# A hybrid recurrence, attention and gating block: scores on row halves of the array, normalisation after all heads, and sums that stay in PSUM

## The chip, the cores and the metric

The kernel runs on one core of a Trainium2 chip. The metric is the device time of one launch in microseconds (us). The kernel before takes 1037.99 us, the median of three runs (1035.18 to 1039.12). The profiled execution took 1038.81 us; its span, from the first to the last recorded instruction, is 1037.0 us. The engines are TensorE (PE, with its weight loads as PEld), VectorE (DVE), ScalarE (ACT), GpSimd (POOL) and SyncE (SP), which here only issues transfers.

## The reference

One layer of a backbone over 512 latent tokens `x` and 256 context tokens, all of width 1024 and in float32. Both are modulated by a small network of the condition vector, and one projection makes the inputs of three branches:

```python
px = split_proj(modulate(x, sh_x, sc_x), w_in, b_in)          # 512 x 12288; pc: the same of ctx
# A: a convolution of width 4, then a gated linear recurrence over tokens in both directions
h_a = rglru_scan(conv(px[0]), ..., reverse=False) + rglru_scan(conv(px[0]), ..., reverse=True)
# B: differential attention, 8 heads, two maps (m) of 64 channels each, rotary q and k
s = einsum('bqhmd,bkhmd->bhmqk', q, k) * 64 ** -0.5           # k: 512 latent + 256 context
p = softmax(s)
o = einsum('bhqk,bkhe->bqhe', p[:, :, 0] - lam * p[:, :, 1], v)
attn = o * rsqrt(mean(o * o) + eps) * g * 0.2                 # mean over a head's 128 channels
# C: spatial gating of u = px[6] by layer_norm(v = px[7])
sgu = u * (w_s @ layer_norm(v) + b_s)
y = sum(sigmoid(gate_i) * ((branch_i * silu(g_i)) @ w_branch[i]) for i in A, B, C)
x_new = layer_norm(alpha * x + gt_x * (y @ w_out))
```

## The kernel before

**Numbers.** Every projection is done to float32 accuracy out of three passes of a faster format: an operand is kept as a rounded part (hi) and the rest (lo), and `mm3` (lines 57 to 64) issues hi by hi, hi by lo and lo by hi for each of 8 slices of 128 along the contraction. Its three matmuls are the lines L62, L63 and L64 of the profile. The modulated latents `xhl` and the context `chl` stay in SBUF in this form. Making hi is a cast on ScalarE, lo a subtraction on VectorE or GpSimd.

**Weights.** They stream through in units. SyncE issues a transfer of 512 KB into one of three buffers `raw`, ScalarE casts it to hi (L121), and GpSimd during attention, VectorE otherwise, subtracts to lo (L122), into one of four slots `w`. A channel-major unit (`cm`) is 128 output channels by all 1024 inputs and takes one slot: its product has channels in partitions and 512 tokens in columns, 24 matmuls of 512 columns. A token-major unit (`tm`) is 256 output channels and takes two slots: tokens lie in partitions, and each of four token tiles takes 24 matmuls of 256 columns into one accumulator. A unit's slot is filled again by `pump` after a unit is used.

**Order.** TensorE's instructions run in the order in which the code issues them. For the other engines and the transfers a scheduler places each instruction by its estimate of when it can start, with priority for what stands under `high_priority`; `order` and `issue_after` tie a few of ScalarE's to one another. PSUM is used as two accumulators of 512 columns (`acc`) and three tiles of 1024 (`big`).

**Stages.** Head and modulation (0 to 62 us); the values of the first heads and attention (62 to 412); the recurrence of branch A together with branch B's output projection (412 to 645); branch C's `sv` (645 to 703); then A's output, `u`, the spatial gating, C's output, the gate row `gr`, and `out` with the last layer norm.

**Attention** has 32 steps, 8 heads by 4 tiles of 128 queries. A step issues `scores` (L705: for each map a `big` tile of 128 queries by 768 keys), `softmax` (row maxima L715 on VectorE, exponentials L720 on ScalarE, the second of them written over its own score tile in PSUM), `combine` (L730, the difference of both maps), the transposes of the step before (L735) with their split (L746, L748), and in between projections from a table `fill`: k, the context's k, q, v and the gate `gb` of later heads. For each head `values` multiplies with v and `rms` normalises: `ms` is the mean of the squares over 128 channels, by a matmul with a matrix of 1/128, and L762 to L764 take logarithm, exponential and product. Small work for the next head (the rotary product, whose one factor GpSimd multiplies, and the splits of q and k) waits in a list of chores, and `drain` issues some of it in each step.

For the scores, q and k of a head lie as 128 partitions, 64 for each map. `qd` and `kd` hold for each map hi in one half of the partitions and lo in the other; q's hi and lo are copied into the other half as well, by a transfer that GpSimd issues. So two matmuls with a contraction of 128 give the three products of a map.

**Recurrence.** Group g of 128 channels takes `xa` (512 latents) and `xac` (256 context tokens) into the padded row `pad`, a convolution on VectorE (`xc`), its split (`xch`, `xcl`), four gate products `ri` with sigmoids, the decay and scans, then `ga`; `branch_a` writes the result to DRAM (`pa_d`). Branch B's split output `hsB` is multiplied in `merge_b` (`y1`), gated by `merge_gate` (`gt1`). After the loop `pa` is read back for branch A.

**Branch C.** `proj_tokens` makes `sv` and `u`: a product of 24 matmuls, and then a sum with the bias on VectorE (L1041) that empties the accumulator. The bias is a row copied to all partitions by a transfer.

## Time and profile before

| | |
|---|---|
| Median of three runs | 1037.99 us (1035.18 to 1039.12) |
| Profiled execution | 1038.81 us, span 1037.0 us |
| Mean granted clock of TensorE | 0.972 of full speed |
| Busy: TensorE, VectorE, ScalarE, GpSimd | 94%, 64%, 51%, 15% of the span |

A row of a timeline gives the start, the duration and the operation, outputs before the arrow; in brackets stands how long the engine had been idle and who released it. A matmul's duration includes its way through a pipeline, so what it costs is read from the distance between two starts. The granted clock is a share of full speed: 1.0 is 2.4 GHz, 0.5 is 1.2.

### The profile page before, as it was taken

What the parts mean: (1) busy time and instruction counts of PE and PEld (TensorE: products, weight loads), DVE (VectorE), ACT (ScalarE), POOL (GpSimd) and SP (SyncE); (2) the same over time, 40 slices, a digit from 0 to 9 for tenths busy, and PEclk for the clock granted to TensorE, in tenths of its full rate; (3) what the DMA queues carried; (4) which work ended last, traced back from release to release, by engine and by line L of the source; (5) the groups of instructions that cost most, each with busy time, mean ns of one, the idle gap of its engine ahead of it and who ended that gap; (6) DMA issues with size and microseconds to landing.
All of it is one profiled execution on the core that took longest, in us unless ns stands there. A gap on an engine that the chain in (4) does not pass through costs nothing.

```text
span 1037.0 us, 14225 instructions
## 1 busy us (share of the span) xinstructions
PE 974.0 (94%) x5719; PEld 844.0 (81%) x5719; DVE 663.6 (64%) x1024; ACT 526.1 (51%) x741; POOL 155.7 (15%) x117
## 2 busy tenths in 40 slices
PE   5997799989989998999999999599999999999996
PEld 4796688878878886888888888598889988888896
DVE  4479788788788663787777776348433356424567
ACT  3145856647647796897777794213231234332221
...
GB/s 299 296 103 84 62 61 21 42 101 21 41 102 21 41 102 70 43 51 102 102 102 92 82 92 92 189 107 132 95 99 82 82 102 82 236 171 145 98 61 82
DMA packets 148184, 103.41 MB, mean 100 GB/s; under 512 B 3629, under 2 KB 143382, under 8 KB 148118
## 3 DMA queue, kind: packets, MB, share of 16 engines
...
q10 hardware_dynamic: 144, 0.10, 0.0%
...
## 4 chain that ended last, share of the span: by engine, by line
PE 66%; DVE 16%; ACT 10%; DMA 4%; issue 3%; SPq 1%; POOL 0%; POOLq 0%; ACTq 0%; DVEq 0%
PE y L62 4%; PE gt L62 4%; PE gt L64 4%; PE gt L63 4%; PE y L64 4%; PE y L63 4%; DVE mxn L715 2%; DVE e L730 2%; DVE kd L565 2%; PE out L62 1%; PE u L62 1%; PE u L64 1%; PE u L63 1%; PE out L64 1%; PE out L63 1%
## 5 line engine op out<-in xcount | busy, mean ns | idle before, releaser
L121 ACT CAST w<-raw 128x1024 fp32r<-128x1024 f32 x96 | 99.7, 1044 | 83.5 <-PE y L64 20.0
L122 DVE TENSOR_TENSOR w<-raw,w 128x1024 fp32r<-128x1024 f32 x71 | 86.4, 1222 | 66.9 <-ACT w L121 66.9
L62 PE MATMUL gt<-xhl,w 128*128 128x512 f32 x192 | 75.6, 394 | 1.3 <-ACT pad L865 1.3
L63 PE MATMUL gt<-xhl,w 128*128 128x512 f32 x192 | 74.8, 390 | 0.0
L64 PE MATMUL gt<-xhl,w 128*128 128x512 f32 x192 | 74.8, 390 | 0.0
L705 PE MATMUL s<-kd,qdq 128*128 128x512 f32 (+1 forms) x256 | 58.7, 368 | 15.6 <-ACT e L720 6.0
L122 POOL TENSOR_TENSOR w<-raw,w 128x1024 fp32r<-128x1024 f32 x25 | 61.0, 2445 | 67.4 <-ACT w L121 67.4
L705 PEld LDWEIGHTS s<-kd,qdq 128*128 128x128 f32 x256 | 44.5, 196 | 27.1 <-issue 12.7
L715 DVE TENSOR_REDUCE mxn<-s 128x1 f32<-128x768 f32 x64 | 58.3, 949 | 7.5 <-PE s L705 7.5
L720 ACT ACTIVATE e<-s,mxn 128x768 f32<-128x768 f32 x32 | 28.8, 900 | 50.9 <-DVE mxn L715 50.8
...
L62 PEld LDWEIGHTS gt<-xhl,w 128*128 128x128 f32 x192 | 36.1, 188 | 9.1 <-ACT pad L865 1.5
L64 PEld LDWEIGHTS gt<-xhl,w 128*128 128x128 f32 x192 | 36.0, 188 | 7.7
L63 PEld LDWEIGHTS gt<-xhl,w 128*128 128x128 f32 x192 | 36.1, 188 | 7.0
...
L730 DVE SCALAR_TENSOR_TENSOR e<-s,sm,e 128x768 f32<-128x768 f32 x32 | 32.6, 1017 | 6.5 <-ACT e L723 5.7
L54 ACT CAST vh<-v 128x128 fp32r<-128x128 f32 x48 | 12.4, 264 | 42.7 <-PE v L64 19.5
L842 ACT ACT_TABLE_LOAD x25 | 32.1, 1283 | 0.5
L62 PE MATMUL xa<-xhl,w 128*128 128x512 f32 x64 | 26.3, 411 | 4.8 <-ACT pad L865 4.8
L748 DVE TENSOR_TENSOR wtl<-t,wth 128x768 fp32r<-128x768 f32 x32 | 30.3, 950 | 0.6 <-ACT wth L746 0.5
L723 ACT ACTIVATE e<-e,sm 128x768 f32<-128x768 f32 x32 | 29.9, 934 | 0.2 <-DVE sm L722 0.2
L842 ACT ACTIVATE rt<-ri,colB 128x770 f32<-128x770 f32 x32 | 27.7, 906 | 2.5 <-PE ri L64 1.8
...
## 6 DMA issues: line engine op xcount, KB each, us to landing
raw<-in_w_in_dram SPq DMA_DIRECT2D x96, 512.0 KB, 3.9
raw<-in_w_branch_dram SPq DMA_DIRECT2D x24, 512.0 KB, 4.0
...
qdq<-qdq POOLq DMA_DIRECT2D x16, 256.0 KB, 3.2
adg<-in_w_ada_dram SPq DMA_DIRECT2D x8, 512.0 KB, 6.6
raw<-in_w_out_dram SPq DMA_DIRECT2D x8, 512.0 KB, 3.4
xtok<-in_x_dram SPq DMA_DIRECT2D x4, 512.0 KB, 5.7
ada<-in_w_ada_dram SPq DMA_DIRECT2D x4, 512.0 KB, 5.9
```

Of the source, the lines that this page charges most:

```text
L62: PE.matmul(ps, ah, bh, start=(first and i == 0), stop=False)
L63: PE.matmul(ps, ah, bl, start=False, stop=False)
L64: PE.matmul(ps, al, bh, start=False, stop=(last and i == n - 1))
L121: S.copy(h, raws[j])
L122: state["lo"].tensor_tensor(l, raws[j], f(h), ALU.subtract)
L705: PE.matmul(sp[:, sl], qds[h][:, 2 * m + j, qs], kds[h][:, m, sl], start=(j == 0), stop=(j == 1))
L715: V.tensor_reduce(mxn[:, m:m + 1], sps[m][:, 0:TA], mybir.AxisListType.X, ALU.max, negate=True)
L720: S.activation(e, sps[m][:, 0:TA], AF.Exp, bias=mxn[:, m:m + 1], accum_out=sm[:, m:m + 1])
L723: S.mul(es[i][0], es[i][0], sm[:, 0:1])
L730: V.scalar_tensor_tensor(e0, e1, sm[:, 1:2], e0, op0=ALU.mult, op1=ALU.add)
L748: V.tensor_tensor(wts[h][1][:, :, qs], src, f(wts[h][0][:, :, qs]), ALU.subtract)
L842: order[0] = S.activation(out, in_, fn, **kw)
```

## The change

- *Scores.* q and k are kept as hi and lo over all 128 partitions. A map's three products are separate matmuls on its own 64 rows of the array (`tile_position`), the two maps alternating: 12 matmuls a step where 8 were. The copies of q by transfers and the splits by halves go: a head's k and q are cast by ScalarE and subtracted by VectorE in one piece each. The rotary product of GpSimd goes to VectorE.
- *Softmax.* Both exponentials are written to SBUF.
- *Normalisation and gates.* `gb`'s sigmoid becomes a hyperbolic tangent and a linear step. `rms` leaves only the mean of squares, on 32 output columns, and copies it to `msb`. After the last head one logarithm and one exponential work on all heads; the result goes to DRAM (`rs_d`), is read back spread over all partitions (`rsb`, five groups of transfers through two buffers), and multiplied into `ob` by VectorE, ahead of the splits to `hsB`. `ob` is evicted by ScalarE.
- *Pools.* SBUF for attention is in three pools (`mp`, `a1`, `at`). `a1` is released at step 28, and `pad`, the recurrence's weights and `xc` take its place (`l1`), so that group 0 is prepared before the last values.
- *Recurrence.* `gt1` comes ahead of the gates (group 0) or behind them, `y1` between the two directions' gates.
- *Token-major projections.* `sv`, `u` and the first half of `out` use 512 columns and weight units of 512 by 512, half of the contraction each. The sums of four token tiles stay in two `big` tiles over both halves. The bias of `sv` is loaded ahead of `pa`, and the split of `hsA` is tied to places in `sv`.

Where instructions stand, in three places. First, VectorE at the change of attention from step 11 to 12, where the k of the fourth head is split (`kd` from the latent k `zk` and the context k `zc`; `e` is the combine, `wtl` the split of transposed weights, `mxn` the maxima, `vl` the split of values). Before:

```order
L730 SCALAR_TENSOR_TENSOR e_11_1838<-s_1_1830,sm_1835,e_11_1838 128x768
L570 TENSOR_TENSOR kd_1845<-zk_1810,kd_1845 64x512
L748 TENSOR_TENSOR wtl_1718<-t_1879,wth_1717 128x6x128
L565 CAST kd_1845<-zc_1877 64x256 x2
L570 TENSOR_TENSOR kd_1845<-zk_1810,kd_1845 64x512
L715 TENSOR_REDUCE mxn_1939<-s_0_1928 128x1
L715 TENSOR_REDUCE mxn_1939<-s_1_1933 128x1
L570 TENSOR_TENSOR kd_1845<-zc_1877,kd_1845 64x256
```

After:

```order
L739 SCALAR_TENSOR_TENSOR e_11_1873<-e_11_1876,sm_1870,e_11_1873 128x768
L757 TENSOR_TENSOR wtl_1748<-t_1914,wth_1747 128x6x128
L582 TENSOR_TENSOR kd_1881<-zk_1841,kd_1881 128x512
L582 TENSOR_TENSOR kd_1881<-zc_1912,kd_1881 128x256
L55 TENSOR_TENSOR vl_1313<-v_5_1925,vh_1312 128x128
L55 TENSOR_TENSOR vl_1380<-v_5_1925,vh_1379 128x128
L726 TENSOR_REDUCE mxn_1975<-s_0_1960 128x1
L726 TENSOR_REDUCE mxn_1975<-s_1_1961 128x1
```

The casts have left VectorE, and two subtractions over 128 partitions stand for four over 64. Second, SyncE's transfers where the recurrence ends and `sv` begins (`bvv` is the bias, `lg` a row of the layer norm). Before:

```order
L103 DMA raw_0_5665<-in_w_in_dram 128x4x256
L1026 DMA pa<-pa_d 128x512 x8
L1031 DMA bvv<-in_b_in_dram 128x1024
L1031 DMA lg<-in_sgu_ln_g_dram 128x1024
L1068 DMA wsall<-in_sgu_w_dram 128x8x128
```

After:

```order
L109 DMA raw_1_5754<-in_w_in_dram 128x2x512
L109 DMA raw_0_5770<-in_w_in_dram 128x2x512
L1067 DMA bvv<-in_b_in_dram 128x1024
L1074 DMA pa<-pa_d 128x512 x7
L1067 DMA lg<-in_sgu_ln_g_dram 128x1024
L109 DMA raw_1_5812<-in_w_in_dram 128x2x512
```

The bias stands ahead of `pa`, and the eighth part of `pa` has gone to GpSimd's queue. Third, VectorE at the start of the recurrence, between the convolution of group 1 (`xc`) and its split (`xcl`; `rt` are gate products, `lwl` the split of the gate weights). Before:

```order
L55 TENSOR_TENSOR hsB<-ob,hsB 128x512 x4
L871 TENSOR_SCALAR xc_3876<-pad,colB 128x770
L874 SCALAR_TENSOR_TENSOR xc_3876<-pad,colB,xc_3876 128x770
L122 TENSOR_TENSOR w_3977<-raw_3659,w_3977 128x1024
L874 SCALAR_TENSOR_TENSOR xc_3876<-pad,colB,xc_3876 128x770 x2
L897 TENSOR_TENSOR rt_3897<-rt_3897,xc_3786 128x770
L897 TENSOR_TENSOR rt_3917<-rt_3917,xc_3786 128x770
L854 TENSOR_TENSOR lwl_3932<-lw_3795,lwh_3931 128x512
L909 SCALAR_TENSOR_TENSOR rt_3888<-a_3925,rt_3888 128x770
L882 TENSOR_TENSOR xcl_3939<-xc_3876,xch_3938 128x770
```

After:

```order
L916 TENSOR_TENSOR ob<-ob,rsb_4073 128x512
L828 SCALAR_TENSOR_TENSOR xc_3966<-pad,colB,xc_3966 128x770
L55 TENSOR_TENSOR hsB<-ob,hsB 128x512
L916 TENSOR_TENSOR ob<-ob,rsb_4087 128x512
L916 TENSOR_TENSOR ob<-ob,rsb_4064 128x512 x2
L938 TENSOR_TENSOR rt_4019<-rt_4019,xc_3845 128x770
L938 TENSOR_TENSOR rt_4039<-rt_4039,xc_3845 128x770
L916 TENSOR_TENSOR ob<-ob,rsb_4078 128x512 x2
L807 TENSOR_TENSOR lwl_4055<-lw_3902,lwh_4053 128x512
L950 SCALAR_TENSOR_TENSOR rt_4010<-a_4047,rt_4010 128x770
L916 TENSOR_TENSOR ob<-ob,rsb_4092 128x512
L923 TENSOR_TENSOR xcl_4061<-xc_3966,xch_4060 128x770
```

The products with `rsb`, which wait for transfers, stand among the gates' work and ahead of the split of group 1.

The diff, cut to its core; `conv`, `conv_in`, `lru_w` and `pad` moved up to where `l1` is known, with `l1` for `lr`:

```diff
+    def proj_th(ps, X, tt, W, half):
+        mm3(ps, X, W, [np.s_[:, 4 * half + k, tt * P:(tt + 1) * P] for k in range(4)],
+            [np.s_[:, k, :] for k in range(4)], half == 0, half == 1)
...
+        elif kind != "tm":
+            raw = wp.tile([P, 2, 512], F32, tag="raw", bufs=3, name=f"raw{i}_{part}")
+            r0 = 512 * int(kind[1]) + 256 * part
+            nc.sync.dma_start(raw, src[r0:r0 + 256, c0:c0 + 512]
+                              .rearrange("(k p) c -> p k c", p=P))
...
-        want("tm", win, 7 * D + j * CW)
+    def want_th(src, c0):
+        for n in range(2):
+            want(f"t{n}", src, c0, (2 * n, 2 * n + 1))
...
+    mp = tc.alloc_tile_pool(name="mp", bufs=1, side="right", reuse_waits="tile")
+    a1 = tc.alloc_tile_pool(name="a1", bufs=1, side="right", reuse_waits="tile")
     at = tc.alloc_tile_pool(name="at", bufs=1, reuse_waits="tile")
-    ropc = at.tile([P, T], F32, name="ropc")
-    rops = at.tile([P, T], F32, name="rops")
+    msb = mp.tile([P, 2, T], F32, tag="msb", name="msb")
...
-            G.tensor_tensor(z, z, ropc, ALU.mult)
-        chore(0.6, name, c0)
+            V.tensor_tensor(z, z, ropc, ALU.mult)
...
-            qds[h] = at.tile([P, 4, T], F32R, tag="qd", bufs=2, name="qd" + n)
+            qds[h] = at.tile([P, 2, T], F32R, tag="qd", bufs=2, name="qd" + n)
+            S.mul(qds[h][:, 0, :], z, 0.125)
+
+        def lo():
             qd = qds[h]
...
-            qd = qds[h]
-            a, b = slice(64 * m, 64 * m + 64), slice(64 - 64 * m, 128 - 64 * m)
-            V.scalar_tensor_tensor(qd[a, 2 * m + 1, :], z[a], 0.125, f(qd[a, 2 * m, :]),
+            V.scalar_tensor_tensor(qd[:, 1, :], z, 0.125, f(qd[:, 0, :]),
                                    op0=ALU.mult, op1=ALU.subtract)
...
+        chore(0.1, n, hi, 4 * h - 5)
+        chore(0.7, n, lo)
 
     def k_split(n, h, z, sl):
-
         def hi():
             if h not in kds:
                 kds[h] = at.tile([P, 2, TA], F32R, tag="kd", bufs=2, name=f"kd{h}")
+            S.copy(kds[h][:, 0, sl], z)
...
-        def lo(m):
-            kd = kds[h]
-            a, b = slice(64 * m, 64 * m + 64), slice(64 - 64 * m, 128 - 64 * m)
-            V.tensor_tensor(kd[b, m, sl], z[a], f(kd[a, m, sl]), ALU.subtract)
+            V.tensor_tensor(kd[:, 1, sl], z, f(kd[:, 0, sl]), ALU.subtract)
...
+        chore(0.1, n, hi, 4 * h - 5)
+        chore(w + 0.15, n, lo)
...
-            S.activation(sg, ps, AF.Sigmoid, bias=bcol(40 + i))
+            S.activation(sg, ps, AF.Tanh, bias=hb[:, i:i + 1], scale=0.5)
+            S.activation(sg, sg, AF.Identity, bias=halfc, scale=0.5)
...
-        sps = []
-        for m in range(2):
-            sp = big_t(f"s{i}_{m}")
-            for sl in (slice(0, 512), slice(512, TA)):
-                for j in range(2):
-                    PE.matmul(sp[:, sl], qds[h][:, 2 * m + j, qs], kds[h][:, m, sl],
-                              start=(j == 0), stop=(j == 1))
-            sps.append(sp)
+
+        sps = [big_t(f"s{i}_{m}") for m in range(2)]
+        for sl in (slice(0, 512), slice(512, TA)):
+            for j, (jq, jk) in enumerate(((0, 0), (0, 1), (1, 0))):
+                for m in range(2):
+                    a = slice(64 * m, 64 * m + 64)
+                    PE.matmul(sps[m][:, sl], qds[h][a, jq, qs], kds[h][a, jk, sl],
+                              start=(j == 0), stop=(j == 2), tile_position=(64 * m, 0))
...
-            e = sps[1][:, 0:TA]
-            if m == 0:
-                e = at.tile([P, TA], F32, tag="e0", bufs=2, name=f"e0_{i}")
+            e = at.tile([P, TA], F32, tag=f"e{m}", bufs=2 - m, name=f"e{m}_{i}")
...
-        with hp(0):
+        with hp(1):
             V.tensor_tensor(wts[h][1][:, :, qs], src, f(wts[h][0][:, :, qs]), ALU.subtract)
...
-        sq = at.tile([P, T], F32, tag="sq", bufs=1, name=f"sq{h}")
+        sq = mp.tile([P, T], F32, tag="sq", name=f"sq{h}")
         S.activation(sq, ps, AF.Square, bias=vbias[:, h:h + 1])
-        V.tensor_scalar(ob[:, h, :], ps, vbias[:, h:h + 1], gcol, op0=ALU.add, op1=ALU.mult)
+        S.activation(ob[:, h, :], ps, AF.Identity, bias=vbg[:, h:h + 1], scale=gcol)
...
     def rms(h, sq):
-        pm = (acc_t if h < 7 else big_t)(f"ms{h}")[:, 0:T]
-        PE.matmul(pm, ones, sq, start=True, stop=True)
-        S.activation(sq, pm, AF.Ln, bias=epst)
-        S.activation(sq, sq, AF.Exp, scale=-0.5)
-        G.tensor_tensor(ob[:, h, :], ob[:, h, :], sq, ALU.mult)
+
+        pm = (acc_t if h < 7 else big_t)(f"ms{h}")
+        r = slice(32 * (h % 4), 32 * (h % 4) + 32)
+        PE.matmul(pm[r, 0:T], ones[:, 0:32], sq, start=True, stop=True,
+                  tile_position=(0, 32 * (h % 4)))
+        order[0] = S.copy(msb[r, h // 4, :], pm[r, 0:T])
...
+        if i == 28:
+            a1.release()
+            l1 = tc.alloc_tile_pool(name="l1", bufs=1, side="right", reuse_waits="tile")
+            lru_dma(0)
+            pad = pad_alloc()
         pump()
     drain(99)
     after_scores(31, sqs)
-    ps0 = acc_t("xa0")
     W = w_next()
-    proj_cm(ps0, W, X, 0, T)
+    ps = acc_t("xa0")
+    proj_cm(ps, W, X, 0, T)
     pump()
+    with tc.high_priority():
+        conv_in(0, ps, True)
+    ps = acc_t("xac0")
+    proj_cm(ps[:, 0:TC], W, C, 0, TC)
+    with tc.high_priority():
+        conv_in(0, ps[:, 0:TC], False)
+        conv(0)
+        lru_hi(0)
     sqs.append((7, values(7, big_t)))
-    ps1 = acc_t("xac0")
-    proj_cm(ps1[:, 0:TC], W, C, 0, TC)
     finish(sqs)
+
+    def act(out, in_, fn, **kw):
+
+        with tc.issue_after(order[0].ins):
+            order[0] = S.activation(out, in_, fn, **kw)
+
+    dr = ctx.enter_context(tc.tile_pool(name="dr", bufs=1, space=bass.MemoryType.DRAM))
+    rs_d = dr.tile([H, T], F32, name="rs_d")
+    act(msb, msb, AF.Ln, bias=epst)
+    act(msb, msb, AF.Exp, scale=-0.5)
+    for h in range(H):
+        r = 32 * (h % 4)
+        G.dma_start(rs_d[h:h + 1, :], msb[r:r + 1, h // 4, :])
     at.release()
...
+    def hs_b(n, hs_):
+
+        rsb = mp.tile([P, len(hs_), T], F32, tag=("sq", "msb")[len(hs_) - 1], name=f"rsb{n}")
+        for j, h in enumerate(hs_):
+            nc.sync.dma_start(rsb[:, j, :], rs_d[h].partition_broadcast(P))
+        for j, h in enumerate(hs_):
+            V.tensor_tensor(ob[:, h, :], ob[:, h, :], rsb[:, j, :], ALU.mult)
+            split(hs[:, 0, h, :], hs[:, 1, h, :], ob[:, h, :])
...
+        if i == 0:
+            merge_gate(0)
         if i < 8:
             gates(i, 0)
         if i > 0:
-            merge_gate(i - 1)
+            merge_b(i - 1)
         if i < 8:
             gates(i, 1)
+            if i > 0:
+                merge_gate(i)
             decay(i)
         if i < 7:
             lru_w(i + 1)
             conv_split(i + 1)
-        if i > 0:
-            merge_b(i - 1)
+        if i == 0:
+            for n, hs_ in enumerate(((0, 1), (2,), (3, 4), (5,), (6, 7))):
+                hs_b(n, hs_)
+            macc = gp.tile([P, KT, T], F32, tag="h", name="macc")
...
-    pa = g3.tile([P, KT, T], F32, tag="h2", name="pa")
-    hsA = g2.tile([P, 2, KT, T], F32R, tag="hs", name="hsA")
-    for g in range(8):
-        nc.sync.dma_start(pa[:, g, :], pa_d[g])
-
...
-    def proj_tokens(dst, bias, name):
-        for j in range(4):
-            W = w_next()
-            for tt in range(4):
-                ps = acc_t(f"{name}{j}_{tt}")
-                proj_tm(ps[:, 0:CW], X, tt, W)
-                pump()
-                V.tensor_tensor(dst[:, tt, j * CW:(j + 1) * CW], ps[:, 0:CW],
-                                bias[:, j * CW:(j + 1) * CW], ALU.add)
+    bvv = bcast(b_in[0, 7 * D:8 * D], "bvv")
+    pa = g3.tile([P, KT, T], F32, tag="h2", name="pa")
+    hsA = g2.tile([P, 2, KT, T], F32R, tag="hs", name="hsA")
+    for g in range(7):
+        nc.sync.dma_start(pa[:, g, :], pa_d[g])
+    G.dma_start(pa[:, 7, :], pa_d[7])
...
+    def proj_tokens(dst, bias, name, then=None):
+
+        for j in range(2):
+            cs = slice(j * 512, j * 512 + 512)
+            bk = [big_t(f"{name}{j}_{t}") for t in range(2)]
+            for half in range(2):
+                W = w_next()
+                for tt in range(4):
+                    ps = bk[tt // 2][:, tt % 2 * 512:tt % 2 * 512 + 512]
+                    proj_th(ps, X, tt, W, half)
+                    pump()
+                    if half == 1:
+                        done = V.tensor_tensor(dst[:, tt, cs], ps, bias[:, cs], ALU.add)
+                if then is not None:
+                    then(2 * j + half, done if half else None)
...
+    def hs_a(step, done):
+
+        if step != 1:
+            return
+        with tc.issue_after(state["hi"].ins):
+            for g in range(8):
+                S.copy(hsA[:, 0, g, :], pa[:, g, :])
+        with tc.issue_after(done.ins):
+            for g in range(8):
+                V.tensor_tensor(hsA[:, 1, g, :], pa[:, g, :], f(hsA[:, 0, g, :]), ALU.subtract)
+
+    proj_tokens(vz, bvv, "sv", hs_a)
...
+    bk = [big_t(f"out{t}") for t in range(2)]
+    for half in range(2):
         W = w_next()
...
-                outp(tt, j, W)
+            ps = bk[tt // 2][:, tt % 2 * 512:tt % 2 * 512 + 512]
+            proj_th(ps, M, tt, W, half)
+            pump()
+            if half == 1:
+                residual(tt, 0, 512, ps, 0)
```

## Rows read from the trace of the kernel before

**Rows 1.** The page's first part: engine, busy us, share of the span, instructions.
```profile
PE 974.0 (94%) x5719; PEld 844.0 (81%) x5719; DVE 663.6 (64%) x1024; ACT 526.1 (51%) x741; POOL 155.7 (15%) x117
```

**Rows 2.** Windows: stretch, us; PE, PEld, DVE, ACT, POOL; clock, DMA, GB/s.
```profile
62.00:200.00 138.00, 123.73 (x723) 108.49 (x722) 113.68 (x209) 85.71 (x144) 52.20 (x32) 0.96 0.25 69
200.00:300.00 100.00, 92.26 (x537) 80.97 (x536) 84.58 (x141) 61.01 (x105) 38.35 (x22) 0.93 0.21 59
300.00:412.00 112.00, 108.68 (x605) 92.39 (x604) 70.68 (x127) 80.60 (x122) 37.29 (x23) 1.00 0.20 57
412.00:445.00 33.00, 28.69 (x142) 24.21 (x143) 24.70 (x30) 28.07 (x38) 2.75 (x2) 0.90 0.19 56
643.00:704.00 61.00, 49.34 (x391) 48.93 (x390) 27.74 (x44) 11.98 (x16) 0.54 (x1) 0.89 0.42 134
```

**Rows 3.** TensorE's waits, 62 to 445: who for whom, us, times, longest.
```profile
PE v L62 <- DVE vl L55: 6.8, 5, 4.7
PE s L705 <- ACT e L720: 6.0, 3, 2.2
PE s L705 <- issue: 5.4, 1, 5.4
...
PE s L705 <- DVE e L730: 4.3, 4, 1.9
```

**Rows 4.** ScalarE's groups, 62 to 412: line, xcount, busy us, mean ns, idle before.
```profile
L670 ACT ACT_TABLE_LOAD x8 | 10.3, 1283 | 0.1
L762 ACT ACT_TABLE_LOAD x8 | 10.3, 1283 | 0.1
```

**Rows 5.** Timeline of VectorE, 203 to 217: start, us, line, operation.
```profile
205.32 3.92 DVE L565 CAST kd<-zc 64x256 fp32r<-64x256 f32 x2
...
211.96 1.81 DVE L715 TENSOR_REDUCE mxn<-s 128x1 f32<-128x768 f32 x2
```

**Rows 6.** Timeline of GpSimd, the same stretch.
```profile
206.65 4.84 POOL L122 TENSOR_TENSOR w15l<-raw,w15h 128x1024 fp32r<-128x1024 f32 x2
```

**Rows 7.** Timeline of TensorE, 655 to 668 (idle before and releaser in brackets).
```profile
661.12 0.58 PE L62 MATMUL sv<-w60h,xhl 128*128 128x256 f32 x1 [11.66 <-DVE vz L1041]
...
665.54 0.28 PE L64 MATMUL sv<-w60h,xhl 128*128 128x256 f32 x1
665.66 0.28 PE L62 MATMUL sv<-w60h,xhl 128*128 128x256 f32 x1
```

**Rows 8.** Timeline of SyncE's DMA queue, 643 to 656.
```profile
647.43 6.76 SPq L1026 DMA_DIRECT2D pa<-pa_d  x8
```

**Rows 9.** Timeline of TensorE, 620 to 640.
```profile
620.98 0.39 PE L62 MATMUL ga<-xhl,w 128*128 128x512 f32 x1
...
626.42 0.39 PE L62 MATMUL gt<-xhl,w 128*128 128x512 f32 x1
```

**Rows 10.** The page's costliest groups: xcount, busy, mean ns, idle and its releaser.
```profile
L720 ACT ACTIVATE e<-s,mxn 128x768 f32<-128x768 f32 x32 | 28.8, 900 | 50.9 <-DVE mxn L715 50.8
```

**Rows 11.** The chain of waits, 354 to 357: start, us, what.
```profile
354.75 1.40 PE s L705 x8
```

**Rows 12.** Timeline of TensorE, 950 to 953.2 (the second `gr` row ends the first).
```profile
950.29 0.39 PE L64 MATMUL y<-hsC,w 128*128 128x512 f32 x1
950.61 1.95 PE L1156 MATMUL gr<-adg,w32o 128*32 128x128 f32 x64
...
951.94 0.62 PE L1156 MATMUL gr<-adg,w32o 128*32 128x128 f32 x16
952.49 0.50 PE L62 MATMUL y<-hsC,w 128*128 128x512 f32 x1
952.83 0.40 PE L63 MATMUL y<-hsC,w 128*128 128x512 f32 x1
```

**Rows 13.** The DMA view: issue, queue, xcount, KB each, us to landing.
```profile
pa_d<-ha POOLq DMA_DIRECT2D x8, 256.0 KB, 2.3
bu<-in_b_in_dram SPq DMA_DIRECT2D x1, 512.0 KB, 3.6
```

185 lines of the change are left out of this document (83 added, 102 removed).

## The prediction

> **What bounds the kernel now.** I read four views: the page's engine line, then windows by stage, then TensorE's waits, then the timeline at the places those name. TensorE (PE) is busy 94% of the span [rows 1], so two things only can change the time: the columns it streams, and the places where it stands still or runs at 1.2 GHz instead of 2.4. The windows [rows 2] find these places. Over the attention loop with its start (62 to 412 us) PE idles 14.3 + 7.7 + 3.3 = 25.3 us; the granted clock of 0.96 and 0.93 there means 2 x (0.04 x 138 + 0.07 x 100) = 25 us at half rate, worth at most 12 more, so the loop loses 25 to 37 us of 350. From 412 to 445, where attention hands over to the recurrence, it loses 4.3 idle and up to 3.3 by the clock. From 643 to 704 it idles 11.7. The head before 62 us and the tail behind the last matmul are not touched.
>
> The waits say what was late [rows 3]. The score matmuls `s` waited 15.7 us: 6.0 for an exponential on ScalarE, 4.3 for the combine of line 730, 5.4 with nothing named. The second score tile stays in PSUM until the combine has read it (the exponential overwrites it there), so all of these are late softmax steps. Two causes show. ScalarE reloads its table, 1.28 us each time, for the normalisation of each head and for each `gb` gate, 8 and 8 [rows 4], and nearly every one is followed by a load back: some 30 loads, 38 us of ScalarE. And VectorE stands still on SBUF work while GpSimd runs: two casts of 64 x 256 took 3.92 us [rows 5], across a GpSimd pair of subtractions of 4.84 us [rows 6], and the maximum that softmax needs is queued behind them and starts at 211.96.
>
> **The change, part by part.** The sum is made against the profiled execution's 1038.8 us (span 1037.0 plus 1.8 around it), 0.8 above the median of the runs.
>
> 1. *Bias load ahead of `pa`.* The 11.66 us wait of `sv` [rows 7] ends with the bias add L1041. The bias DMA stood behind eight `pa` loads, whose issue took 6.76 us from 647.43 on [rows 8], since the last one's source had first to be written. Now bias stands ahead, and the first half's sums need no bias at all. With the wait go the 21 matmuls at 1.2 GHz behind it: 4.42 us for 21 steps of 0.12 = 2.52 [rows 7], 1.9 us. Together 13.6; I take 13, since the weights might be next late: -13 (bounds -14 and -8).
>
> 2. *512 columns instead of 256.* A 512-column step is 0.227 us (24 of them from 620.98 to 626.42), a 256-column one 0.12 [rows 7, 9]. `sv` and `u` each turn 384 steps into 192: 46.1 - 43.6 = 2.5 us; half of `out` 1.3. This is on the path, as PE is saturated there: -6.
>
> 3. *Stalls of the loop.* Thirty table loads leave; the extra ScalarE work (a second pass for the sigmoid, three casts, one eviction and a 32-row copy per head, each well under 1 us) costs less than they did. On VectorE a head's q and k work falls from 19 instructions to 11, though the rotary product comes over from GpSimd. Both score tiles are now released by the exponentials, not by the combine: in a set, two maxima of 0.9 and two exponentials of 0.9 [rows 5, 10] end some 3 to 3.5 us behind the scores, while PE has 2.9 to 5.4 us of projections and six transposes behind them. So the 10.3 us of named softmax waits should mostly go, with the clock drops they cause. Left over are blocks by GpSimd (it still splits weights, two SBUF subtractions of VectorE stand where six did) and the `v` waits (6.8, most at the start). I let 12 of the 37 us stay: -25 (bounds -37 and 0; what is late next is the maximum behind a blocked subtraction).
>
> 4. *Scores on half the rows.* A set was 8 matmuls, 1.40 us [rows 11]. It becomes 12, over 64 rows each, in pairs on the two halves of the array. No row shows two row halves. The nearest is `gr`, four column strips at once: its 32 matmuls (64 records, the last 16 from 951.94 on) run from 950.61 to 952.49, 1.88 us [rows 12], about 0.12 per four. If a pair runs so too, a set is 3 x (0.23 + 0.12) = 1.05. But `gr` also paid to get in and out: 0.32 instead of 0.23 before it; behind it 0.34 for a step of 0.23, and 0.2 for the last four, which start near 952.28, where 0.11 was due [rows 12]; 0.3 in all. So 1.05 + 0.30 = 1.35: 32 x -0.05 = -2 (bounds -11 with a free entry, +31 if the halves go one after the other).
> The section Key Properties of the Trainium skill's page TensorEngine Tiling (Array Packing) says that changing the tiling mode drains TensorE, and a change of tile within a mode does not. It speaks against this part; `gr`'s 0.3 us agrees with it. By the rule the gain of 11 us is nearly all given back; without it the term would be -11 and the time 983.
>
> 5. *`ms` on 32 columns* streams as long as before and pays the exit eight times: +2 (0 to +3).
>
> 6. *Hand-over.* Lost now: up to 7.6. `pad` and the gate weights get their own space before attention ends, so the wait of `xa` and the three products in front of the gates cover the convolution. New: `ms` of the last head follows its values directly and waits about 1.2 us for the square; then logarithm and exponential of all heads, a write to DRAM and five broadcasts back through two buffers. From the end of the last values: 2.9 to the copy, two table loads and two passes of about 1.1 (estimate) with a cast between, 8.5; eight writes issued by GpSimd at 0.5 and landing in 2.3 [rows 13]; then four rounds of broadcast (2.8 to 3.6 each, by the 3.6 of `bu` [rows 13]) and products, in VectorE's queue between the convolution of group 1 and its split. That split is done near 31 us; PE, with xa, xac, gt, the gates of group 0, xa and xac (26 us) behind 2.2 us of `ms`, asks near 28.5. So some 3 us of wait there and 2 at the last `hsB`: -7 + 1 + 5 = -1 (bounds -7, +8). Queued behind those waiting products are the gates' own multiplications, and ScalarE's first cast of `hsB` stands ahead of the first sigmoids.
>
> Sum: -13 - 6 - 25 - 2 + 2 - 1 = -45, near 993; I say **992**.
>
> **Rivals.**
> *B, the weights of a pair load in turn.* Every 256-column step of 0.12 holds one load, so a pair could cost 0.24 whatever its width: 6 x 0.24 + 0.3 = 1.74, +11 instead of -2: 1005. For: the four loads of `gr` were of 32 columns, here two of 128. Against: `gr`'s loads did not add up. Chance 0.14.
>
> *C, the halves go one after the other:* 6 x (0.23 + 0.12) + 0.3 = 2.4, +32: 1026. For: no row shows rows halved. Against: the column strips overlapped. 0.12.
>
> *D, the loop stays bound by VectorE behind GpSimd.* The combine now reads both inputs from SBUF, where before one came from PSUM; if it and the k subtractions meet GpSimd's 2.4 us splits [rows 6] as the casts did [rows 5], the maximum behind them is as late as now, and half to all of part 3 is lost: 1005 to 1017. Against: the combine ends before the split of the same step starts, and transposes need it a step later. 0.10.
> The page SBUF — State Buffer of the Trainium skill, in Who interferes with whom, says that a VectorE instruction with two SBUF inputs contends with a GpSimd one that reads SBUF, and that the loser blocks for the whole of it. Rows 5 and 6 agree; that the combine is a new loser rests on the page alone.
>
> *E, slower.* Every change of row half inside a set drains the array as leaving `gr` did: 12 x 0.2 + 2.1 + 0.3 = 4.8 us, +109: near 1100. It decides from 2.8 us a set on (1.40 + 45/32). For: nothing here shows a change of row half. Against: `gr` changes strips every 7 to 90 ns. 0.05.
>
> *F, the hand-over waits 15 us rather than 5*, if each broadcast round costs double: 1004. 0.05. That the change doesn't do what it says is excluded for the loads: ScalarE's order has none between the start of attention and the last normalisation.
>
> **How the numbers follow.** The forecast has 0.54, and by itself 974 (stalls gone, entry free) to 1002. Going up through B, F, D and C, the range is 970 to 1026; outside are E and some of the edges. Half a per cent of this kernel (5.2 us) is what a measurement can tell from no change. All cases but E lie below 1033; allowing for two going wrong together: faster 0.91, same 0.03, slower 0.06.
>
> **What would show it.** Parts 1 and 2: `sv` starts with no wait over 1 us, at clock 1.0, and `sv` plus `u` last about 87 us. Part 3: from 62 us to the first `xa` PE idles under 12 us and ScalarE loads no table. Part 4: pairs of `s` start within 20 ns and a set lasts about 1.35 us; 1.7, 2.4 or over 2.8 say B, C or E. Part 6: `ri` of group 1 waits about 3 us for `xcl`. The prediction is wrong if a set exceeds 2 us, if the combine takes 2 us often, or if the recurrence starts with waits over 10 us.

## The result and the profile after

The changed kernel takes 1045.13 us (median of four runs, 1044.97 to 1045.5), the kernel before 1038.55 in the same study: ratio 1.0067, 95% interval 1.005 to 1.0084. It is slower by 6.6 us where I had forecast 46 us faster. The first part of the page, and then TensorE's windows over the stretches of [rows 2]:

```profile
PE 974.4 (93%) x5367; PEld 807.5 (77%) x5367; DVE 639.4 (61%) x955; ACT 500.8 (48%) x734; POOL 111.8 (11%) x86
```

```profile
62.00:200.00 138.00, 128.71 (x801) 109.18 (x800) 108.32 (x200) 76.31 (x143) 29.41 (x13) 0.95 0.18 54
200.00:300.00 100.00, 92.45 (x583) 77.23 (x582) 75.87 (x120) 58.49 (x108) 25.48 (x11) 0.98 0.18 53
300.00:412.00 112.00, 106.95 (x624) 86.72 (x625) 67.90 (x110) 69.06 (x117) 28.21 (x14) 1.00 0.18 52
412.00:445.00 33.00, 26.75 (x142) 22.84 (x140) 21.21 (x29) 25.29 (x33) 4.32 (x8) 0.95 0.30 89
643.00:704.00 61.00, 50.64 (x209) 39.83 (x210) 33.22 (x45) 15.19 (x20) 1.63 (x3) 0.94 0.47 147
```

Over the whole span VectorE, ScalarE and GpSimd all have less to do than in [rows 1], and TensorE is busy as long as before. Cut by the first matmul of each stage in the timeline instead of at fixed times, the stages are (us):

| | `v` to first `xa` | to `sv` | `sv` | to `u` | `u` | to `out` | `out` to the end |
|---|---|---|---|---|---|---|---|
| before | 333.5 | 247.8 | 59.9 | 88.2 | 46.1 | 144.2 | 55.1 |
| after | 331.5 | 261.0 | 51.0 | 88.1 | 49.1 | 144.1 | 56.0 |

So three things have to be explained: attention gained 2.0 us, not the 25 of parts 3 to 5; the recurrence with its hand-over lost 13.2; `sv`, `u` and `out` gained 5.0 of 19. The 2.0 us are made of two parts. Up to the first score 6.1 us were gained, most of it one wait of 4.7 us of `v` that is gone; from the first score to the first `xa` the time grew from 304.3 to 308.3 us. TensorE's waits of the changed kernel, in the loop of attention (85 to 394) and then behind it (412 to the end):

```profile
PE o L63 <- DVE wtl L757: 11.5, 6, 2.2
PE s L717 <- ACT e L729: 5.2, 3, 4.0
PE v L62 <- DVE vl L55: 3.9, 3, 1.3
```

```profile
PE ga L62 <- DVE ha L986: 6.0, 1, 6.0
PE sv L62 <- DVE vz L1091: 4.4, 4, 1.5
PE u L62 <- DVE u L1091: 4.2, 4, 1.5
PE y L62 <- ACT pad L819: 3.9, 1, 3.9
PE ri L63 <- DVE xcl L923: 3.5, 1, 3.5
PE out L62 <- DVE tm L1250: 2.2, 2, 1.5
```

The scores wait 5.2 us where they waited 15.7 [rows 3], but the values `o` now wait 11.5 us for the split `wtl`, about 2 us in each of six heads. Behind the loop, the waits of `ga` and `u`, and that of `y` for `pad`, are new; `ri` and `out` had waited 0.2 us each, and `sv` once, 11.7 us, for the bias. One of the waits for `wtl`, on three engines (VectorE, GpSimd, TensorE; idle time in brackets):

```profile
210.24 0.75 DVE L550 STREAM_SHUFFLE t1q<-zq 128x512 f32<-128x512 f32 x1
211.02 2.51 DVE L551 TENSOR_TENSOR zq<-zq,ropc 128x512 f32<-128x512 f32 x1
213.45 0.68 DVE L553 TENSOR_TENSOR t1q<-t1q,rops 128x512 f32<-128x512 f32 x1
214.06 0.94 DVE L757 TENSOR_TENSOR wtl<-t,wth 128x768 fp32r<-128x768 f32 x1
214.92 0.94 DVE L726 TENSOR_REDUCE mxn<-s 128x1 f32<-128x768 f32 x1
```

```profile
210.58 2.40 POOL L134 TENSOR_TENSOR w<-raw,w 128x1024 fp32r<-128x1024 f32 x1 [1.41 <-ACT w L133]
```

```profile
212.82 0.39 PE L62 MATMUL o<-wth,vh 128*128 128x512 f32 x1
215.06 0.50 PE L63 MATMUL o<-wtl,vh 128*128 128x512 f32 x1 [1.84 <-DVE wtl L757]
```

The rotary product that came to VectorE takes 2.51 us: it starts while GpSimd subtracts a weight and ends 0.55 us behind it. `wtl` stands two places behind the product in VectorE's queue. My first theory: this product, the shared PSUM tiles of `sv`, `u` and `out`, the place of `gt1`, and `rsb` are the four losses.

### The profile page after: what moved, and what is told of

Its sections match the earlier page's. It is cut to its first block, busy times and chain, and to the rows that moved or that the text cites. A ratio compares the mean times of both kernels' runs of the same rounds, so it can differ in the third digit from the quotient of the medians.

```text
span 1043.2 us, 13356 instructions
## 1 busy us (share of the span) xinstructions
PE 974.4 (93%) x5367; PEld 807.5 (77%) x5367; DVE 639.4 (61%) x955; ACT 500.8 (48%) x734; POOL 111.8 (11%) x86
## 4 chain that ended last, share of the span: by engine, by line
PE 66%; DVE 17%; ACT 8%; DMA 5%; issue 2%; SPq 0%; POOL 0%; POOLq 0%; DVEq 0%; ACTq 0%
PE gt L62 4%; PE gt L63 4%; PE gt L64 4%; PE y L62 4%; PE y L63 4%; PE y L64 4%; ACT e L729 3%; DMA ada<-in_w_ada_dram 2%; DVE mxn L726 2%; DVE zq L551 2%; PE s L717 1%; PE gc L62 1%; PE gc L64 1%; PE out L62 1%; PE gc L63 1%
## 5 line engine op out<-in xcount | busy, mean ns | idle before, releaser
L729 ACT ACTIVATE e<-s,mxn 128x768 f32<-128x768 f32 x64 | 57.5, 901 | 74.8 <-DVE mxn L726 74.8
L134 POOL TENSOR_TENSOR w<-raw,w 128x1024 fp32r<-128x1024 f32 x25 | 59.9, 2400 | 224.3 <-ACT w L133 222.6
L717 PE MATMUL s<-kd,qdq 64*128 64x256 f32 (+1 forms) x384 | 44.6, 358 | 5.2 <-ACT e L729 5.2
L717 PEld LDWEIGHTS s<-kd,qdq 64*128 64x128 f32 x384 | 32.9, 188 | 20.8 <-issue 9.6
L739 DVE SCALAR_TENSOR_TENSOR e<-e,sm,e 128x768 f32<-128x768 f32 x32 | 32.6, 1019 | 12.0 <-ACT e L732 11.4
L63 PE MATMUL o<-wtl,vh 128*128 128x512 f32 x48 | 21.5, 448 | 11.5 <-DVE wtl L757 11.5
L62 PE MATMUL ga<-xhl,w 128*128 128x512 f32 x64 | 25.8, 404 | 6.0 <-DVE ha L986 6.0
L62 PE MATMUL y<-hsB,w 128*128 128x512 f32 x64 | 25.9, 405 | 3.9 <-ACT pad L819 3.9
```

The lines of the kernel that those rows point to most:

```text
L62: PE.matmul(ps, ah, bh, start=(first and i == 0), stop=False)
L63: PE.matmul(ps, ah, bl, start=False, stop=False)
L134: state["lo"].tensor_tensor(l, raws[j], f(h), ALU.subtract)
L717: PE.matmul(sps[m][:, sl], qds[h][a, jq, qs], kds[h][a, jk, sl], start=(j == 0), stop=(j == 2), tile_position=(64 * m, 0))
L729: S.activation(e, sps[m][:, 0:TA], AF.Exp, bias=mxn[:, m:m + 1], accum_out=sm[:, m:m + 1])
L739: V.scalar_tensor_tensor(e0, e1, sm[:, 1:2], e0, op0=ALU.mult, op1=ALU.add)
```

## Experiments

All ratios are against the kernel before, run in the same study.

**Order of token tiles.**
```diff
-                for tt in range(4):
+                for tt in (0, 2, 1, 3):       # the same in out
                     ps = bk[tt // 2][:, tt % 2 * 512:tt % 2 * 512 + 512]
```


> The changed kernel with one edit: the four token tiles of sv, u and the first half of out are worked in the order 0, 2, 1, 3. Theory: tiles 0 and 1 (and 2 and 3) share one PSUM tile of 1024 columns, so the first matmul of tile 1 waits until VectorE has read tile 0 out of the same PSUM tile; ten such waits of 0.95 to 1.6 us, 12 us with the step behind each. With neighbours in different PSUM tiles they go: sv 51.0 to about 45.5 us, u 49.1 to 44, out shorter by 2.5; the kernel 1045 to 1033. Rival: the waits are for the bias add as such or for a free PSUM tile (three in the ring); then the order changes nothing, 1045.


1031.87 us, ratio 0.9929 (0.9913 to 0.9944). The stages became 45.3 (`sv`), 43.6 (`u`) and 53.2 (`out` to the end). All ten waits of the changed kernel for a sum (four of `sv`, four of `u`, two of `out`) are gone. In the changed kernel two of the four of `sv` read:

```profile
671.88 0.50 PE L62 MATMUL sv<-w61h,xhl 128*128 128x512 f32 x1 [1.47 <-DVE vz L1091]
678.40 0.50 PE L62 MATMUL sv<-w61h,xhl 128*128 128x512 f32 x1 [0.78 <-DVE vz L1091]
```

These are the first matmuls of token tiles 1 and 3, held until VectorE has read tile 0 or 2 from the other half of the same PSUM tile. The theory holds in size and in place: 13.3 us below the changed kernel, 12 expected.

**`gt1` of group 7 behind `ga` of group 6.** Its weight unit moves with it.
```diff
+        if i == 8:
+            merge_gate(7)
         if i > 0:
             merge_b(i - 1)
         if i < 8:
             gates(i, 1)
-            if i > 0:
+            if 0 < i < 7:
                 merge_gate(i)
```


> The changed kernel with one edit: the last gate product gt1 of group 7 goes back behind ga of group 6 (its place in the kernel before), its weight with it. Theory: ahead of the decay it holds back ScalarE, whose sigmoid of gt1 stands before the decay's exponentials, by 6.5 us, so that the last scan is late and ga of group 7 waits 6.1 us for an accumulator and then runs at half clock; with gt1 as cover the wait and the 1.26 us before gt1 go: 1045 to about 1036. Rival: the end of the recurrence is bound by the scans of VectorE themselves; then the wait moves to the gt1 or y1 behind it and the time stays within 2 us of 1045.


1039.66 us, ratio 1.001 (1.0 to 1.002): 5.5 us below the changed kernel, of the 9 expected. First `xa` to `sv` fell from 261.0 to 255.0; `ga` waits 1.1 us instead of 6.0, and `y1` in front of it 2.0 where it had not waited. In the changed kernel ScalarE's waits from 620 to 650 have this line:

```profile
ACT sgm L890 <- PE gt L64: 6.5, 1, 6.5
```

The sigmoid of `gt1` precedes the decay in ScalarE's chain, so the last decay, the last scan, and the accumulator that `ga` needs were late by that.

**Rotary product back on GpSimd.**
```diff
-            V.tensor_tensor(z, z, ropc, ALU.mult)
-        chore(1.3, name, c0)
+            G.tensor_tensor(z, z, ropc, ALU.mult)
+        chore(0.6, name, c0)          # the weight of this chore for drain
```


> The changed kernel with one edit: the rotary product by the cosine goes back from VectorE to GpSimd. Theory: on VectorE it stands ahead of the split wtl and takes 2.5 us when GpSimd splits a weight at the same time, so the values of every head wait 2.0 us for wtl (12.5 us in all, and half-rate stretches behind some of them); with the product on GpSimd these waits go and the loop from the first score to the first xa falls from 308 to about 295 us: the kernel 1045 to about 1031. Rival: wtl is late for the casts of ScalarE or because VectorE is full; then another instruction stands in its place, the values still wait 2 us a head, and the time stays near 1045.


1054.46 us, ratio 1.0157 (1.014 to 1.0174): 9 us above the changed kernel, so the theory that the product's place on VectorE is the cause fell. The waits of `o` for `wtl` grew:

```profile
PE o L63 <- DVE wtl L757: 20.0, 6, 3.5
```

VectorE and then GpSimd in this kernel:

```profile
217.46 2.82 DVE L554 TENSOR_TENSOR zq<-zq,t1q 128x512 f32<-128x512 f32 x1 [1.19 <-POOL zq L551]
220.20 0.94 DVE L757 TENSOR_TENSOR wtl<-t,wth 128x768 fp32r<-128x768 f32 x1
```

```profile
215.63 1.80 POOL L551 TENSOR_TENSOR zq<-zq,ropc 128x512 f32<-128x512 f32 x1 [1.89 <-DVE t1q L550]
217.39 2.35 POOL L134 TENSOR_TENSOR w<-raw,w 128x1024 fp32r<-128x1024 f32 x1
```

Now VectorE's next step, the sum, waits for GpSimd's product and is then held by the weight subtraction that GpSimd does behind it. What was common to both is the weight subtraction.

**These three with the split of group 1 given priority.**
```diff
-            lru_w(i + 1)
-            conv_split(i + 1)
+            with hp(i == 0):
+                lru_w(i + 1)
+                conv_split(i + 1)
```


> The changed kernel with the three edits together (order of token tiles 0, 2, 1, 3; gt1 of group 7 behind ga of group 6; rotary product on GpSimd) and a fourth: the split of group 1 of the recurrence gets high priority, so that it stands ahead of the last products with rsb. Theory: the four causes are apart from each other, so their gains add: 12 + 9 + 14 + 3.7 = 39, 1045 to about 1007. Rival: they cover one another (a stall taken away is taken up by the next late one): less than half of it, 1025 or more.


1036.22 us, ratio 0.9978 (0.9966 to 0.9989). The rotary loss is in it again (waits of `o`: 20.0). The priority removed the wait of `ri` for `xcl`, but `y1` of group 0 waits 8.5 us instead of 5.1 in the run of `gt1` alone: from first `ri` to `sv` both take about 227 us, so the priority gained nothing.

**`wtl` products last.** `values` issues the twelve products with `wth`, then the six with `wtl`.


> The changed kernel with one edit: in the values of a head the six products with the rest of the weights (wtl) come last, behind the twelve with wth, so that wtl is asked for 2.7 us later. My theory of the rotary product fell in part (with the product on GpSimd VectorE waited for GpSimd and was then blocked by the next weight split, and the waits grew to 3.3 us a head); what is left of it: wtl stands in VectorE's queue behind rotary work that GpSimd's weight splits block, and the values ask for it 4.4 us behind its transposes. Then the waits of 2.0 us go, and with them the stretches at half clock: the loop from first score to first xa 308 to about 294 us, the kernel 1045 to 1031. Rival: the next late thing takes the place (scores waiting for the softmax, as VectorE is late for those too): the loop stays above 303 us, 1040 or more.


1053.39 us, ratio 1.0129 (1.0107 to 1.0151): the expectation missed, and its rival missed the place. `o` waits no more; `v` does:

```profile
PE v L62 <- DVE vl L55: 10.4, 3, 3.5
PE v L62 <- ACT ob L769: 8.8, 3, 3.2
```

The first line is a split on VectorE itself. In the second, `v` needs an accumulator that ScalarE empties into `ob`; in the trace that stands behind exponentials which had waited 4.7 us for a maximum of VectorE. So the lateness is VectorE's in both, and the order of the matmuls decides which of them shows it.

**Scores alone, in the kernel before.** `hi`, `lo`, `k_split` and `scores` of the change, all else as before.


> The kernel before with the scores' part of the change alone: q and k as hi and lo over 128 partitions (casts on ScalarE, subtractions on VectorE), twelve matmuls on row halves; the copies of q by transfers go, the rotary product stays on GpSimd, all else is before's. Theory: a set costs about 1.45 us with its way in and out (0.09 before, 0.2 and 0.1 behind) against 1.40, so the part alone gives nothing on TensorE; less work on VectorE and fewer GpSimd issues may take away a few of the waits of the scores: 1030 to 1040 (before 1038). Rival: the row halves bring the 11 us that the streams save and the loop lost them elsewhere: 1027 or less.


1045.33 us, ratio 1.0063 (1.0038 to 1.0088): a loss of 6, outside what I expected. The six waits of `o` for `wtl` come with the scores' part alone, on code whose rotary product never left GpSimd (beside them `gb` waits 3.9 us once, which it does not in the kernel before):

```profile
PE o L63 <- DVE wtl L729: 10.2, 6, 2.0
PE s L687 <- DVE e L711: 7.6, 7, 2.8
```

In front of `wtl` stands the rotary sum. It waits for GpSimd's product and is then held by the weight subtraction that GpSimd does next, in all six heads (one of them, VectorE and then GpSimd; idle time in brackets):

```profile
181.82 2.87 DVE L525 TENSOR_TENSOR zq<-zq,t1q 128x512 f32<-128x512 f32 x1 [1.18 <-POOL zq L522]
184.61 0.94 DVE L729 TENSOR_TENSOR wtl<-t,wth 128x768 fp32r<-128x768 f32 x1
```

```profile
181.74 2.39 POOL L122 TENSOR_TENSOR w<-raw,w 128x1024 fp32r<-128x1024 f32 x1
```

**Bias ahead of `pa` alone, in the kernel before.**


> The kernel before with the bias of sv loaded ahead of the eight pa loads, and nothing else. Theory (part 1 of the prediction): the wait of 11.7 us in front of the second group of sv goes and the half-rate stretch with it: sv 60.0 to about 46.5 us, the kernel 1038 to 1025. Rival: the weights of sv or the accumulators are next late, and at least half of the wait stays: 1032 or more.


1033.61 us, ratio 0.9932 (0.9908 to 0.9956): 6 to 7 us, half of the forecast. Of the wait 6.9 us stay. The bias is issued at 647.07, behind a load of weights that waits for its buffer, and the eight `pa` loads follow at once; the first sum with the bias starts at 655.64, 8.6 us behind the issue (that the `pa` loads slow it is likely, but no run separates it):

```profile
635.72 11.30 SPq L103 DMA_DIRECT2D raw<-in_w_in_dram  x3
647.07 0.50 SPq L1025 DMA_DIRECT2D bvv<-in_b_in_dram  x1
647.75 8.33 SPq L1032 DMA_DIRECT2D pa<-pa_d  x8
```

In the changed kernel the bias is issued at 658.51 and the first sum that needs it starts only at 671.14, 12.6 us later, for the first half of the contraction needs no bias. That is what saves the rest there.

**Four edits together** (token tiles, `gt1`, `wtl` last, `y1` of group 0 behind both gates).


> The changed kernel with four edits: token tiles in the order 0, 2, 1, 3; gt1 of group 7 behind ga of group 6; wtl products last in the values; y1 of group 0 behind both directions' gates of group 1 instead of between them (2.1 us more work in front of its wait). Theory: 13 (measured alone) + 6 (measured alone) + 14 + 2 = 35, 1045 to about 1010. Rival: the loop's gain does not come: 1024.


1033.22 us, ratio 0.9934 (0.9908 to 0.9959): the expected 1010 did not come. `wtl` last made attention longer again (337.2 us from `v` to `xa`, 331.5 in the changed kernel), and with `y1` moved the gates `ri` wait 5.1 us for ScalarE where `y1` had waited for `pad`.

**Weight subtractions on VectorE.** The second theory: it is GpSimd's weight subtraction that holds VectorE.
```diff
-    state["lo"] = G
+    state["lo"] = V        # during attention
     for _, u in units("v", 0):
```


> The changed kernel with one edit: during attention the lo parts of the weights (25 subtractions of 128 x 1024) are made by VectorE instead of GpSimd. Theory: in every head GpSimd's weight subtractions of 2.4 us block VectorE (36 us in all in this loop, as many as before the change) at the rotary work of q and at the context k; what is queued behind (wtl, the maxima, so the exponentials and ScalarE's evictions) is late, and TensorE stops wherever it first needs one of them: at the scores in the kernel before, at the values in the changed one, at v when the values ask later. With GpSimd out of the way VectorE takes 30 us more work but loses the 36: the waits for wtl go, the loop from first score to first xa falls from 308 to about 296, the kernel 1045 to about 1032. Rival: VectorE's own work bounds the loop; 30 us more of it make it longer, 1050 or more.


1022.63 us, ratio 0.9841 (0.9827 to 0.9856), 22.5 below the changed kernel: more than expected. The rotary product of q takes 0.69 us in all six heads where it took 2.50 to 2.79 (one line of either, changed kernel first; duration in ns, least, median and most):

```profile
L551 DVE TENSOR_TENSOR zq<-zq,ropc x6: 2504/2772/2790, 131.4 to 329.8; 128x512 f32<-128x512 f32 x6
```

```profile
L551 DVE TENSOR_TENSOR zq<-zq,ropc x6: 693/694/705, 126.8 to 306.5; 128x512 f32<-128x512 f32 x6
```

From first score to first `xa`, changed kernel and then this one (windows):

```profile
85.50:393.80 308.30, 287.19 (x1749) 237.18 (x1749) 222.46 (x367) 182.14 (x325) 72.98 (x34) 0.97 0.16 48
```

```profile
85.80:370.60 284.80, 278.87 (x1749) 231.74 (x1749) 217.14 (x399) 182.55 (x326) 9.02 (x7) 1.00 0.17 51
```

VectorE has 32 instructions more and is busy 5 us less; TensorE idles 5.9 us instead of 21.1, at a granted clock of 1.00 instead of 0.97. That the weights come sooner is not the reason: in this stretch of the changed kernel TensorE never waited for a weight.

**With the other two edits.**


> The changed kernel with three edits: token tiles in the order 0, 2, 1, 3; gt1 of group 7 behind ga of group 6; lo parts of weights by VectorE during attention. Theory: 13 + 6 as measured alone, and 13 from the loop: 1045 to about 1013. Rival (the loop is bound by VectorE's own work): 1030 or more.


1002.9 us, ratio 0.9659 (0.9634 to 0.9683): below the expected 1013, and 36 us below the kernel before. 13.3 + 5.5 + 22.5 = 41.3 from the single runs, 42.2 measured: the causes add.

**No normalisation of branch B.**
```diff
-        rsb = mp.tile([P, len(hs_), T], F32, ...)
-            nc.sync.dma_start(rsb[:, j, :], rs_d[h].partition_broadcast(P))
-            V.tensor_tensor(ob[:, h, :], ob[:, h, :], rsb[:, j, :], ALU.mult)
```


> The changed kernel without the broadcasts rsb and the products with them (branch B is left without its normalisation; logarithm, exponential and the write to DRAM stay). Theory: the waits of ri of group 1 for xcl (3.7 us), of y1 of group 0 (4.2 us) and the half-rate stretches behind them (about 3.5 us) all come from the products that wait for the transfers in VectorE's queue: from the first xa to sv 261 to about 251 us, the kernel 1045 to 1034. Rival: the waits are ScalarE's (two table loads and the casts of hsB ahead of the convolution's input); then less than 4 us go.


1038.97 us, ratio 1.0002 (0.9991 to 1.0012): 6.2 us of the 11 expected. The wait for `xcl` is gone, that of `y1` for `pad` falls from 3.9 to 2.2. The rest is ScalarE's queue, which runs without idle time from 424.9 us to the `pad` that `y1` waits for, at 439.3. From first `xa` to `sv` this run takes 254.4 us, 6.6 less than the changed kernel; with the 6.0 us of `gt1` that makes 12.6 of the 13.2 us that the recurrence lost.

**Second exponential in PSUM again.**
```diff
-            e = at.tile([P, TA], F32, tag=f"e{m}", bufs=2 - m, name=f"e{m}_{i}")
+            e = sps[1][:, 0:TA]
+            if m == 0:
+                e = at.tile([P, TA], F32, tag="e0", bufs=2, name=f"e0_{i}")
```


> The changed kernel with one edit: the second exponential is written over its own scores in PSUM again, as before the change, so that the second score tile is free only after the combine. Theory: the scores' waits fell (19.9 to 6.6 us) because both tiles are free after the exponentials; with the edit they come back, for the combine ends 3 us behind the exponentials, and the loop grows by 5 to 13 us: 1050 to 1058. Rival: the waits fell because ScalarE loads no tables in the loop; then the time stays within 2 us of 1045.


1049.67 us, ratio 1.0102 (1.0087 to 1.0117): 4.5 us above the changed kernel. The scores wait again, 11.5 us for the combine and 4.0 for an exponential, and `o` waits only 1.7 us for `wtl` (`v` waits 7.6 us for its splits, 3.9 in the changed kernel). The waits of the scores and of `o` take each other's place.

**Weight subtractions on VectorE, in the kernel before.**


> The kernel before with one edit: lo parts of the weights by VectorE during attention. Theory: GpSimd's weight subtractions block VectorE there as much as in the changed kernel (35 us), so the edit alone gives the kernel before what it gave the changed one: from the first score to the first xa 304 to about 285 us, the kernel 1039 to 1018 to 1024; the rotary and gate products that stay on GpSimd block less. Rival: before the change table loads and the combine's hold on PSUM were the bound; then less than 8 us go, 1031 or more.


1027.65 us, ratio 0.9887 (0.9867 to 0.9906): between both theories. First `v` to first `xa` is 323.5 us, 10 less. GpSimd was a bound before the change too, but there 9.6 us of waits of `v` for `ob` (line 756 on VectorE) come up:

```profile
PE v L62 <- DVE ob L756: 9.6, 6, 2.1
PE s L705 <- ACT e L720: 2.3, 1, 2.3
```

**The same with the scores' part.**


> The kernel before with lo parts of weights on VectorE and the scores' part of the change (q and k as hi and lo over 128 partitions, twelve matmuls on row halves). Theory: with VectorE free of GpSimd the scores alone are worth what a set is on TensorE, 1.45 against 1.40 us: within 5 us of the run without them in this study. Rival: they gain 11 us by the streams, or cost 6 as they did with GpSimd in the way.


1036.92 us, ratio 0.9993 (0.9977 to 1.0009): 9 us slower than without it; expected was within 5. `o` waits for `wtl` 10.7 us again, now with a weight subtraction and both maxima in front of it in VectorE's queue: in this code, unlike in the changed one, `wtl` has no priority. Nor is GpSimd quite out of the way: beside its rotary product VectorE's weight subtraction takes 2.31 us, 1.23 in the median (VectorE, then GpSimd):

```profile
174.35 2.31 DVE L122 TENSOR_TENSOR w<-raw,w 128x1024 fp32r<-128x1024 f32 x1
```

```profile
173.78 1.80 POOL L522 TENSOR_TENSOR zq<-zq,ropc 128x512 f32<-128x512 f32 x1 [13.96 <-DVE t1q L521]
```

**Table loads back**, with weight subtractions on VectorE: the one-pass sigmoid.


> The changed kernel with lo parts of weights on VectorE, and the gates' sigmoid as one pass again, with its two table loads for each of the eight gates. Theory: 2.6 us of ScalarE for a gate are hidden beside TensorE most of the time when nothing else is late: within 4 us of 1022.6. Rival: table loads are what delays the exponentials (8 gates by 2.6, 21 us): 1035 or more.


1024.22 us, ratio 0.9858 (0.9843 to 0.9873): 1.6 us for 15 table loads, while one pass of ScalarE goes for each of eight gates. With VectorE free the gates' loads are hidden; with VectorE held, and for the loads of the normalisation, no run tried it.

**`ga` of group 0 ahead of `y1` of group 0**, added to the 1002.9 us kernel.


> The kernel of the three edits (1002.9 us) with a fourth: ga of group 0, 5.4 us of TensorE that wait for nothing, goes ahead of y1 of group 0 from the step behind it. Theory: it fills the wait of y1 for the last hsB and the convolution's input (4.6 us, and a half-rate stretch of about 2): 1003 to about 997. Rival: the accumulator that ga holds until the scan is late instead: 1003 or more.


1003.13 us, ratio 0.9651 (0.9634 to 0.9669): no gain. `ga` itself now waits 5.1 us for `pad`, in `y1`'s place.

## Why the prediction was wrong

- *What bounds the kernel.* Right on the places, wrong on the cause of the largest. I read the late softmax as ScalarE's table loads and as VectorE behind GpSimd, and named the loads first, at 38 us of ScalarE. In the one run that tried it, fifteen of them are worth 1.6 us. The rows on the casts held for 3.92 us and on GpSimd's pair [rows 5, 6] showed the bound, and the change leaves GpSimd's weight subtractions where they were. Counted over VectorE's timeline from 62 to 400, instructions that ran over 0.25 us longer than the shortest of their line and shape lost 35 us before, 36 after, and 2 with the subtractions on VectorE.
- *Part 3, -25*: the step that failed is "So the 10.3 us of named softmax waits should mostly go, with the clock drops they cause", taken as time saved. Half of them went: the scores wait no more for the combine, and 5.2 us for an exponential. But a score that waits less only brings TensorE sooner to the next thing that the held VectorE makes, `wtl`, and there it waits 11.5 us. I had named "the maximum behind a blocked subtraction" as next late, and rival D with the combine. The combine took 1.02 us in all 32 steps and never met a subtraction of GpSimd. Of what rival D named, the subtraction of the context k did meet one, 2.42 us in five heads where 0.4 is due, but the waits came from the rotary product, which this very change put onto VectorE, and `wtl` behind it. With the block gone in both, the changed kernel takes 307.8 us from `v` to `xa` and the kernel before 323.5, so parts 3 to 5 were worth 15.7 there, of 25.

  The Trainium skill's page SBUF — State Buffer (Who interferes with whom), which I had cited for the combine alone, says that a VectorE instruction with two SBUF inputs contends with a GpSimd instruction that reads SBUF, and that one with at most one SBUF input does not, outside its 2-port performance modes. The traces agree: the rotary product of q, with two inputs in SBUF, took 2.50 to 2.79 us in all six heads and 0.69 with the block gone; `wtl`, which reads PSUM and SBUF, took 0.95 to 0.96 us also where it ran beside such a subtraction (VectorE, then GpSimd, in the changed kernel):

```profile
353.71 0.96 DVE L757 TENSOR_TENSOR wtl<-t,wth 128x768 fp32r<-128x768 f32 x1 [3.22 <-ACT wth L755]
```

```profile
353.06 2.40 POOL L134 TENSOR_TENSOR w<-raw,w 128x1024 fp32r<-128x1024 f32 x1 [21.00 <-ACT w L133]
```

  The casts of [rows 5] have one input, so they show the blocking only, and not the rule on two inputs with which the prediction says they agree.
- *Part 4, -2*: the pairs do overlap (172 of 192 start within 20 ns); rivals B, C and E are out. A set, in the timeline:

```profile
240.47 0.28 PE L64 MATMUL v<-w15h,xhl 128*128 128x256 f32 x1
240.68 1.33 PE L717 MATMUL s<-kd,qdq 64*128 64x512 f32 x12
241.94 0.50 PE L62 MATMUL q<-xhl,w 128*128 128x512 f32 x1
242.28 0.40 PE L63 MATMUL q<-xhl,w 128*128 128x512 f32 x1
```

  0.09 to get in (0.21 for a step of 0.12), 1.26 for the set with its way out, 0.11 at the next step (0.34 for 0.23): 1.46, against 1.35 forecast and 1.40 before [rows 11]. The entry is paid once more inside the set (the first pair takes 0.33). So +2 instead of -2; the part alone lost 6 and 9 us, and for the rest its waits point to the order on VectorE that comes with it; no run changed the array's part by itself.
- *Parts 1 and 2, -19*: right in size, with one cost missed. With the token tiles apart `sv` fell by 14.6, `u` by 2.5 and the stage of `out` by 1.9, 19.0 in all; the shared PSUM tiles gave 14 of it back. That two accumulations in one PSUM tile wait for each other's reading stood in no term. My test, "`sv` starts with no wait over 1 us", missed by 0.1 us (1.1 us, for the lo part of its first weights), and the waits of up to 1.5 us stood later in `sv`; `sv` plus `u` took 100.1 us, not 87.
- *Part 6, -1*: the wait of `xa` went (first `xa` to first `ri` is 28.5 us with a `gt1` of 5.5 in it, 29.5 before), and `ri` of group 1 waits 3.5 us where I had said 3. Missed: `y1` 3.9 where I said 2, each wait's stretch at 1.2 GHz behind it (the first seven steps behind the wait of `y1` are of 0.43 to 0.58 us where 0.23 is due), and the new place of `gt1`, of which I had weighed only that it covers. Between 446.2 and 621.1 us, where TensorE has other work, no wait over 0.3 us stands; at the last group `ga` waits 6.0.
- *The sum.* Parts 3 to 5 missed by 23 us, parts 1 and 2 by 14, part 6 by 14; any one of them alone would have left the time within 970 to 1026. None of my three signs of being wrong appeared (a set over 2 us, a combine of 2 us, waits over 10 us at the start of the recurrence): they watched the new parts, and the time went in places that I had counted as saved or had not named. Two slips change nothing: a head's q and k work is 18 instructions on VectorE in the trace before, not 19, and with the stalls gone and the entry free the stated terms give 971, not 974.

What stays open: why the scores' part alone made the loop of before longer is shown by its waits and by what stands in front of `wtl`, but not which of its edits brought that order; the remaining wait at the hand-over (about 5 us) moved with every edit and was not removed.
